# Modulation tiles in pairs between the main products of a two-layer streaming encoder, at half as many places

## The chip, the cores and the metric

The kernel runs on one core of one Trainium2 chip. The metric is device time in microseconds (us), from start to end of one launch, as the median of several runs. Inputs and weights lie in the chip's memory (HBM) at the start, outputs at the end.

## The reference

One inference step of two layers over 288 positions (256 of a prompt, 32 of a running stream), 2048 channels, float32. Each layer begins with a normalization whose shift, scale and gate are computed from a condition vector `c`; that computation is the modulation:

```python
def _adaln(x, c, g, w_mod, b_mod):
    mod = jax.nn.silu(c) @ w_mod + b_mod
    shift, scale, gate = jnp.split(mod, 3, axis=-1)
    h = _rmsnorm(x, g) * (1.0 + scale[:, None, :]) + shift[:, None, :]
    return h.astype(x.dtype), gate[:, None, :]

def _attention_layer(x, c, l, ...):
    h, gate = _adaln(x, c, p['norm_g'][l], p['w_mod'][l], p['b_mod'][l])
    proj = h @ p['w_in_att'][ia]
    ...
    x = x + gate * (mixed @ p['w_out_att'][ia])

def _ssm_layer(x, c, l, ...):
    h, gate = _adaln(x, c, p['norm_g'][l], p['w_mod'][l], p['b_mod'][l])
    u, z = jnp.split(h @ p['w_in_ssm'][isd], 2, axis=-1)
    ...
    glu = g * jax.nn.sigmoid(g @ p['w_glu'][isd] + p['b_glu'][isd])
    out = (glu.astype(x.dtype) * jax.nn.silu(z)) @ p['w_out_ssm'][isd]
    x = x + gate * out
```

`w_mod` is 2048 x 6144 for each layer, 96 MB in all, and is multiplied with only two vectors (one for the prompt, one for the stream). The other weight matrices are multiplied with 288 columns each.

## The kernel before

All weights pass through SBUF in tiles of 1 MB (128 x 4 x 512 floats). Two kinds of tiles run on TensorE, and one list, `jobs`, fixes their order:

- A **main** job (`main_job`, L575) multiplies one tile of a weight matrix with the activations. Since float32 weights are too exact for the fast format, each quarter of a tile is split: ScalarE rounds it (`hi`), VectorE forms the rest (`lo`), and TensorE makes three matmuls of 288 columns for each block (`ah,hi`, `al,hi`, `ah,lo`), 48 in all for a tile. The splitting runs ahead of the multiplying by at most `NQ = 8` quarters (`split_step`, L416; `rest_step`, L436).
- A **mod** job (`mod_jobs`, L569) multiplies one tile of `w_mod` with the condition vectors, in plain float32 and without a split: four products that use 32 columns of the array each, side by side (`mod_mm`, L470), recorded as 8 matmuls. 16 such tiles, or 4, form a group that sums into one PSUM bank `mod_ps`. After the last one `mod_fin` (L532) copies the bank out, turns it by 32 small matmuls and adds the bias.

`run_jobs` (L474) walks the list. For a main job it issues the matmuls of the tile, and after every second block it lets quarters be split and takes up to three steps of side work; for a mod job it issues the products, gives the buffer free and takes up to three steps of side work. The order of the loads is that of the list as well: `pump` (L391) issues the next load on SP's queue as soon as one of `NST = 4` buffers is free (the first stage has three more, the last products one more). A mod tile's buffer is free when its products are done, a main tile's when VectorE has formed the last `lo`.

All else, that is attention, the building of the state-space matrices, normalizations and scans, is side work: generators in `Tasks` (L199) whose steps are laid between the matmuls. Whether a step is due is decided while the program is built, from a `Plan` (L39) that adds up estimated durations for each engine and each transfer. On the chip nothing is reordered: every engine, and SP's queue, takes its instructions in the order in which they were laid.

The stages as the list has them: 8 steps `u` with the first three or four attention projections and the modulation of layer 0 in runs of four tiles (L1344); 36 main jobs of the other attention projections (L1365), side by side with attention and with the builder of the state-space matrices; 16 of the output projection (L1408); 32 of the state-space input, without modulation tiles (L1791); 16 of `w_glu` (L1829) and 16 of `w_out_ssm` (L1841). The modulation tiles not needed at once are held in two lists, which the loops of these stages use up:

```python
late = mod_jobs(0, 8, 9, 10, 11) + mod_jobs(1, 0, 1, 2, 3) + mod_jobs(1, 4, 5, 6, 7)   # L1339
last_mods = [j for s in range(8, 12) for j in mod_jobs(1, s)]                          # L1340
```

Four of the 48 tiles in `late` are laid in the last of the 8 steps `u`; the other 44 follow one by one behind the main jobs of L1365 (36) and of the output projection (8). The 16 of `last_mods` follow one by one behind two of every three main jobs of the last two products. Gates of layer 0 are needed first in `op_evac` (L1379), shift and scale of layer 1 in `h1_task` (L1499), and its gates in `fin_evac` (L1821), a quarter of the channels at a time.

Of the kernel before, what the change touches and what calls it, by code (L numbers as in the profile page):

```python
# [271 lines left out]
def build(tc, I, O):  # L272
# [8 lines left out]
    with ExitStack() as ctx:  # L281
# [54 lines left out]
        def need(*keys):  # L336
            side.until(lambda: all(k in ready for k in keys))
# [47 lines left out]
        jobs = []  # L385
# [183 lines left out]
        def mod_jobs(l, *units):  # L569


            m = dict(l=l, s=units, ps=None, begun=set())
            return [dict(kind="mod", mod=m, i=i, src=I["w_mod"][l, units[i // 4], i % 4]) for i in range(4 * len(units))]

        def main_job(wname, block, c, group, stage, first=None, last=None, wide=False, **kw):  # L575

            return dict(kind="main", group=group, chunk=c, stage=stage, src=I[wname][block, c], wide=wide,
                        first=c == 0 if first is None else first, last=c == 3 if last is None else last, **kw)

        def new_group(evac):  # L580
            return dict(ps=[None] * 8, evac=evac)
# [323 lines left out]
        def qkv_evac(kind, b, after):  # L905
            def ev(n, ps, c):
                if n == 0:
                    need(("read", "f", after))
                    qkv_tile(kind, b)
                act.activation(qkv[kind, b][:, n, :], ps, AF.Copy, scale=0.125 if kind == "qd" else 1.0)  # L910
                if n == 3:
                    ready.add((kind, b))
            return ev

        def z_evac(base):
            def ev(n, ps, c):
                k = base + n
                t = sc.tile([128, T], F32, tag="zt", name="zt")
                act.activation(t, ps, AF.Tanh, scale=0.5)
                dve.scalar_tensor_tensor(MX[:, k, :], t, 1.0, ps, op0=ALU.add, op1=ALU.mult)  # L920
                if n == 3:
                    ready.add(("sz", base // 4))
            return ev
# [415 lines left out]
        late = mod_jobs(0, 8, 9, 10, 11) + mod_jobs(1, 0, 1, 2, 3) + mod_jobs(1, 4, 5, 6, 7)  # L1339
        last_mods = [j for s in range(8, 12) for j in mod_jobs(1, s)]  # L1340
# [3 lines left out]
        for u in range(8):  # L1344
            part = starts[:3 + u % 2]
            nxt = mod_jobs(0, u + 1) if u < 7 else late[:len(part)]
            if u == 7:
                late = late[len(part):]
# [16 lines left out]
        for oi, (kd, b) in enumerate(order):  # L1365
            g = new_group(z_evac((0 if kd == "zf" else 8) + 4 * b) if kd[0] == "z" else
                          qkv_evac(kd, b, 0 if oi < 7 else 1))
            for c in range(4):
                jobs.append(main_job("w_in_att", 2 * ATT.index(kd) + b, c, g, "h0"))
                if oi == len(order) - 1:  # L1370
                    jobs[-1]["key"] = ("free", "h0", c)
                jobs += late[:1]
                late = late[1:]

        def op_evac(gi):
            def ev(n, ps, c):
# [31 lines left out]
        for gi, c in [(gi, c) for gi in range(4) for c in range(3)] + [(gi, 3) for gi in range(4)]:  # L1408
            jobs.append(main_job("w_out_att", gi, c, og[gi], "m0", first=c in (0, 3), last=c in (2, 3)))
            if gi == 0:  # L1410
                jobs[-1]["before"] = (lambda c: lambda: need(("m0", c)))(c)
            if gi == 3:
                jobs[-1]["key"] = ("free", "m0", c)
            jobs += late[:1]
            late = late[1:]
        op1 = len(jobs)

        def x_in(gi):
# [386 lines left out]
        def glu_evac(gi):  # L1805
            def ev(n, ps, c):
                k = 4 * gi + n
                need(("sz1", k))
                t = sl.tile([128, T], F32, tag="zt%d" % (k % 2), name="gt")
                act.activation(t, ps, AF.Tanh, scale=0.25, bias=hbglu[:, k:k + 1])  # L1810
                dve.scalar_tensor_tensor(t, t, 1.0, U[:, k, :], op0=ALU.add, op1=ALU.mult)
                TT(SZ[:, k, :], t, SZ[:, k, :], ALU.mult)
                if n == 3:
                    sp.dma_start(MX[:, 4 * gi:4 * gi + 4, :], x1d[:, 4 * gi:4 * gi + 4, :])
                    ready.add(("glu", gi))
            return ev

        def fin_evac(gi):
            def ev(n, ps, c):
                k = 4 * gi + n  # L1820
                need(("mod", 1, 8 + gi))  # L1821
                xk = MX[:, k, :].rearrange("p (s j) -> p s j", s=LC)
                for b, (j0, j1) in enumerate(((0, JP), (JP, NJ))):
                    dve.scalar_tensor_tensor(xk[:, :, j0:j1], ps.rearrange("p (s j) -> p s j", s=LC)[:, :, j0:j1],
                                             gate[:, 1, k, b:b + 1], xk[:, :, j0:j1], op0=ALU.mult, op1=ALU.add)
                squares(k, MX[:, k, :])
            return ev

        for gi in range(4):  # L1829
            g = new_group(glu_evac(gi))  # L1830
            for c in range(4):
                jobs.append(main_job("w_glu", gi, c, g, "g"))
                if gi == 0:
                    jobs[-1]["before"] = (lambda c: lambda: need(("g", c)))(c)
                if gi == 3:
                    jobs[-1]["key"] = ("free", "g", c)
                if 4 * gi + c > 2 and (4 * gi + c) % 3 < 2:
                    jobs += last_mods[:1]
                    last_mods = last_mods[1:]
        l1c = len(jobs)  # L1840
        for gi in range(4):  # L1841
            g = new_group(fin_evac(gi))
            for c in range(4):
                jobs.append(main_job("w_out_ssm", gi, c, g, "m1"))
                if gi == 0:
                    jobs[-1]["before"] = (lambda c: lambda: need(("m1", c)))(c)
                if (4 * gi + c) % 3 < 2:
                    jobs += last_mods[:1]
                    last_mods = last_mods[1:]
        l1d = len(jobs)  # L1850

        side.add(rstd1_task())
# [178 lines left out]
```

## Time and profile before

| what | value |
|---|---|
| median of three runs | 1312.3 us |
| the three runs | 1311.82, 1312.3, 1322.78 us |
| the profiled execution | 1324.34 us, of which the span from first to last instruction is 1322.4 us |
| mean granted clock of TensorE | 0.976 |
| VectorE, ScalarE busy | 69%, 45% of the span |
| moved by DMA | 334.55 MB, mean 253 GB/s |
| matmuls of the main products, by form | 3 x 2304 records, about 300 ns each, started some 0.134 us apart |

A row of a group or of a timeline names the line of the helper that issues the instruction (always L116 here), the engine, the operation, what it writes and reads by the program's names, its shape, and how many instructions it joins. In a timeline the first number is the start in us from the begin of the span, the second the duration, and the brackets at the end hold the idle time of the engine before it and what ended it. PE is TensorE, PEld its weight loads, DVE VectorE, ACT ScalarE; a name with q is the queue that issues transfers. Matmuls overlap in the array, so that costs on TensorE are read from the starts and not from the durations. In a row of windows the stretch and its length are followed by the busy time of each engine, the granted clock, the busy share of the DMA engines and the GB/s.

### The profile page before, as it was taken

What the parts mean: (1) busy time and instruction counts of PE and PEld (TensorE: products, weight loads), DVE (VectorE), ACT (ScalarE), POOL (GpSimd) and SP (SyncE); (2) the same over time, 40 slices, a digit from 0 to 9 for tenths busy, and PEclk for the clock granted to TensorE, in tenths of its full rate; (3) what the DMA queues carried; (4) which work ended last, traced back from release to release, by engine and by line L of the source; (5) the groups of instructions that cost most, each with busy time, mean ns of one, the idle gap of its engine ahead of it and who ended that gap; (6) DMA issues with size and microseconds to landing.
All of it is one profiled execution on the core that took longest, in us unless ns stands there. A gap on an engine that the chain in (4) does not pass through costs nothing.

```text
span 1322.4 us, 27713 instructions
## 1 busy us (share of the span) xinstructions
PE 1245.6 (94%) x11098; PEld 1106.7 (84%) x11098; DVE 912.3 (69%) x2000; ACT 595.2 (45%) x1398; POOL 31.0 (2%) x20
## 2 busy tenths in 40 slices
PE   4999899998999999999999989998999999999996
PEld 2788688887788788877889987987889999999895
DVE  5569987797787779877764883736767685455554
ACT  4533233243354545554653463433536684344441
POOL 0006000000000000000000000000000000000000
PEclk8899999999999999999999989998999999999998
DMA  9878487577978888878966477588756757777631
GB/s 347 369 290 344 184 309 283 190 278 276 314 291 320 305 325 313 327 268 281 358 226 250 129 272 209 163 241 200 220 170 204 218 178 255 254 259 273 228 124 72
DMA packets 114159, 334.55 MB, mean 253 GB/s; under 512 B 47696, under 2 KB 64096, under 8 KB 83312
## 3 DMA queue, kind: packets, MB, share of 16 engines
q1 hardware_dynamic: 101360, 303.14, 66.3%
q10 hardware_dynamic: 12672, 29.65, 6.0%
q8 instruction: 87, 1.43, 0.4%
q14 instruction: 40, 0.33, 0.1%
HBM read 297.69 MB, written 35.06 MB: 252 GB/s over the span
## 4 chain that ended last, share of the span: by engine, by line
issue 48%; PE 25%; DMA 14%; DVE 10%; ACT 1%; SPq 1%; ACTq 0%; POOL 0%; POOLq 0%; DVEq 0%
PE m L116 19%; DMA w<-in_w_in_att 5%; DMA v_d<-v 5%; PE mod_ps L116 3%; DVE v L116 3%; DVE lo L116 2%; DVE tmpv L116 1%; DMA w_d<-W 1%; DMA w<-in_w_wide 1%; DVE dtmp L116 1%; DMA w<-in_w_mod 1%; DVE MX L116 1%; ACT hi L116 1%; SPq L116 1%; PE w_ps L116 1%
## 5 line engine op out<-in xcount | busy, mean ns | idle before, releaser
L116 PE MATMUL m<-ah,hi 128*128 128x288 f32 (+1 forms) x2304 | 713.5, 310 | 12.3 <-DVE qkv L116 6.0
L116 PE MATMUL m<-ah,lo 128*128 128x288 f32 (+1 forms) x2304 | 688.4, 299 | 5.5 <-DVE lo L116 5.4
L116 PE MATMUL m<-al,hi 128*128 128x288 f32 (+1 forms) x2304 | 689.1, 299 | 3.6 <-DVE al L116 3.6
L116 PEld LDWEIGHTS m<-ah,hi 128*128 128x128 f32 x2304 | 440.9, 191 | 74.4 <-issue 39.9
L116 ACT CAST hi<-w 128x512 fp32r<-128x512 f32 x552 | 322.0, 618 | 350.1 <-PE m L116 220.2
L116 DVE TENSOR_TENSOR lo<-w,hi 128x512 fp32r<-128x512 f32 x552 | 366.8, 686 | 148.9 <-ACT hi L116 146.6
L116 PEld LDWEIGHTS m<-ah,lo 128*128 128x128 f32 x2304 | 441.7, 192 | 7.4 <-DVE lo L116 7.3
L116 PEld LDWEIGHTS m<-al,hi 128*128 128x128 f32 x2304 | 442.1, 192 | 4.1 <-DVE al L116 3.8
L116 PE MATMUL mod_ps<-w,cs 128*32 128x512 f32 x744 | 96.9, 614 | 13.5 <-DVE ssq L116 12.6
L116 DVE SCALAR_TENSOR_TENSOR qkv<-m,qkv 128x288 f32<-128x288 f32 x168 | 72.8, 452 | 26.6 <-PE m L116 26.5
L116 DVE TENSOR_TENSOR v<-pt,raw 128x512 f32<-128x512 f32 (+1 forms) x64 | 46.0, 719 | 29.0 <-DMA v_d<-v 24.0
L116 DVE SCALAR_TENSOR_TENSOR MX<-m,gate,MX 128x256 f32<-128x256 f32 x96 | 30.8, 362 | 30.3 <-PE m L116 30.1
L116 PEld LDWEIGHTS mod_ps<-w,cs 128*32 128x32 f32 x744 | 17.0, 109 | 38.9 <-issue 21.4
L116 DVE TENSOR_TENSOR tmpv<-pt,raw 128x512 f32<-128x512 f32 (+1 forms) x64 | 45.9, 717 | 0.0
L116 ACT ACTIVATE yx<-MX 128x288 f32<-128x288 f32 (+1 forms) x38 | 18.8, 495 | 50.9 <-DVE MX L116 50.4
L116 PE MATMUL t_ps<-MX,kb 32*32 32x288 f32 (+7 forms) x1024 | 40.1, 306 | 0.0
L116 PEld LDWEIGHTS t_ps<-MX,kb 32*32 32x32 f32 x1024 | 27.9, 107 | 12.5 <-issue 2.9
L116 DVE SCALAR_TENSOR_TENSOR MX<-MX,c_dT,t_ps 128x288 f32<-128x288 f32 x16 | 8.2, 514 | 42.8 <-PE t_ps L116 42.8
L116 DVE TENSOR_TENSOR v<-v,tmpv 128x512 f32<-128x512 f32 (+1 forms) x48 | 34.3, 714 | 1.7
L116 PE MATMUL y_ps<-Xm,v 128*128 128x74 f32 x256 | 31.9, 279 | 2.6 <-ACT Xm L116 2.6
L116 PEld LDWEIGHTS y_ps<-Xm,v 128*128 128x128 f32 x256 | 30.8, 196 | 3.1 <-ACT Xm L116 2.8
L116 PE MATMUL w_ps<-c_ident,v 128*128 128x128 f32 x128 | 20.4, 283 | 10.4 <-ACT hi L116 2.1
(236 smaller groups left out, 930.4 us busy)
## 6 DMA issues: line engine op xcount, KB each, us to landing
w<-in_w_mod SPq DMA_DIRECT2D x93, 1024.0 KB, 6.0
w<-in_w_in_att SPq DMA_DIRECT2D x40, 1024.0 KB, 8.3
w<-in_w_in_ssm SPq DMA_DIRECT2D x32, 1024.0 KB, 5.9
w<-in_w_wide SPq DMA_DIRECT2D x24, 1024.0 KB, 10.5
w<-in_w_out_att SPq DMA_DIRECT2D x16, 1024.0 KB, 7.1
w<-in_w_glu SPq DMA_DIRECT2D x14, 1024.0 KB, 5.7
w<-in_w_out_ssm SPq DMA_DIRECT2D x12, 1024.0 KB, 5.0
v_d<-v ACTq DMA_DIRECT2D x16, 576.0 KB, 8.7
```

Of the source, the lines that this page charges most:

```text
L116: return f(*a, **k)
```

## The change

The tiles of `late` that remain after the first stage, and those of `last_mods`, are laid two at a time, behind every second main job of the attention projections and the output projection, and behind one of three in the last two products. Which tiles there are, their order among themselves, and all other work stay.

```diff
@@ attention projections (L1368)
                 jobs.append(main_job("w_in_att", 2 * ATT.index(kd) + b, c, g, "h0"))
                 if oi == len(order) - 1:
                     jobs[-1]["key"] = ("free", "h0", c)
-                jobs += late[:1]
-                late = late[1:]
+                if c % 2:
+                    jobs += late[:2]
+                    late = late[2:]
@@ output projection (L1408)
-            jobs += late[:1]
-            late = late[1:]
+            if len(jobs) % 2:
+                jobs += late[:2]
+                late = late[2:]
@@ w_glu (L1829)
-                if 4 * gi + c > 2 and (4 * gi + c) % 3 < 2:
-                    jobs += last_mods[:1]
-                    last_mods = last_mods[1:]
+                if 4 * gi + c > 2 and (4 * gi + c) % 3 == 1:
+                    jobs += last_mods[:2]
+                    last_mods = last_mods[2:]
@@ w_out_ssm (L1841)
-                if (4 * gi + c) % 3 < 2:
-                    jobs += last_mods[:1]
-                    last_mods = last_mods[1:]
+                if (4 * gi + c) % 3 == 1:
+                    jobs += last_mods[:2]
+                    last_mods = last_mods[2:]
```

Written out with M for a main job and m for a modulation tile, the attention projections go from `M m M m M m M m` to `M M m m M M m m`. The list has 138 entries when the output projection begins, so its first main job makes the count odd, and its pairs stand behind its first, third, fifth and seventh main job. In the last two products the pairs stand behind the main jobs 4, 7, 10 and 13 of `w_glu` and 1, 4, 7 and 10 of `w_out_ssm`, counted from 0; before, single tiles stood behind 3, 4, 6, 7, 9, 10, 12, 13, 15 and 0, 1, 3, 4, 6, 7, 9.

## The prediction

> **What bounds the kernel now.** I read the page first, for the busy shares, then the busy time by stage, alone and for the modulation's matmuls (tile mod_ps).
>
> ```profile
> span 1322.4 us, 27713 instructions
> PE 1245.6 (94%) x11098; PEld 1106.7 (84%) x11098; DVE 912.3 (69%) x2000; ACT 595.2 (45%) x1398; POOL 31.0 (2%) x20
> L116 PE MATMUL mod_ps<-w,cs 128*32 128x512 f32 x744 | 96.9, 614 | 13.5 <-DVE ssq L116 12.6 <-DMA w<-in_w_mod 1.0
> ```
>
> TensorE is busy in 94% of the span, so time taken off TensorE is time gained wherever nothing else ends last. The next rows give all engines in three stages; the rows behind the dots give the modulation's matmuls alone.
>
> ```profile
> core 0: us, PE busy (x) PEld busy (x) DVE busy (x) ACT busy (x) POOL busy (x), PEclk, DMA share, GB/s
> 265.00:680.00 415.00, 395.38 (x3309) 334.01 (x3309) 327.85 (x675) 202.65 (x533) 6.00 (x9) 0.99 0.83 301
> 680.00:706.00 26.00, 26.00 (x197) 22.82 (x200) 14.03 (x28) 11.30 (x24) 0.70 (x1) 1.00 0.76 279
> 1100.00:1270.00 170.00, 170.00 (x1349) 153.22 (x1347) 89.19 (x162) 71.75 (x130) 0.00 (x0) 1.00 0.70 250
> ...
> 265.00:680.00 415.00, 43.11 (x320) 0.99 0.83 301
> 680.00:710.00 30.00, 4.26 (x32) 1.00 0.73 262
> 1100.00:1270.00 170.00, 17.04 (x128) 1.00 0.70 250
> ```
>
> A modulation tile is 8 matmuls, so the last three rows hold 320/8 + 32/8 + 128/8 = 40 + 4 + 16 = 60 tiles: exactly those that the change moves. In the last stage and in the short one TensorE never pauses. In the attention stage (265 to 680) it idles 415 - 395.4 = 19.6 us, while the DMA engines are 83% busy: two resources are near their limit there.
>
> **What a lone tile costs, and a row of four.** The TensorE timeline around a lone tile in the last stage, then around a run of four that the first stage already has:
>
> ```profile
> 1114.42 0.29 PE L116 MATMUL m<-ah,lo 128*128 128x288 f32 x1
> 1114.64 1.06 PE L116 MATMUL mod_ps<-w,cs 128*32 128x512 f32 x8
> 1115.63 0.40 PE L116 MATMUL m<-ah,hi 128*128 128x288 f32 x1
> 1115.87 0.29 PE L116 MATMUL m<-al,hi 128*128 128x288 f32 x1
> ...
> 1116.94 0.29 PE L116 MATMUL m<-ah,hi 128*128 128x288 f32 x1
> ...
> 93.89 0.29 PE L116 MATMUL m<-ah,lo 128*128 128x288 f32 x1
> 94.11 3.64 PE L116 MATMUL mod_ps<-w,cs 128*32 128x512 f32 x32
> 97.68 0.40 PE L116 MATMUL m<-ah,hi 128*128 128x288 f32 x1
> 97.92 0.29 PE L116 MATMUL m<-al,hi 128*128 128x288 f32 x1
> ```
>
> Main matmuls start every (1116.94 - 1115.87)/8 = 0.134 us. From the last one before the tile to the second after it pass 1115.87 - 1114.42 = 1.45 us instead of 2 x 0.134, so a lone tile costs 1.18 us. The run of four costs 97.92 - 93.89 - 0.27 = 3.76 us. Each tile behind the first therefore costs (3.76 - 1.18)/3 = 0.86 us: the other 0.32 us belong to leaving the main product and coming back, whatever the number of tiles.
>
> **The change part by part.** No instruction is added or taken away. Moved are 60 tiles, each one load of 1 MB on SP's queue and 8 weight loads and 8 matmuls on TensorE; POOL gets nothing.
>
> *Fewer crossings.* 60 places become 30: 18 in the loop over the attention projections, 4 in the output projection, 8 in the last two products. A pair costs 1.18 + 0.86 = 2.04 us where two lone tiles cost 2.36. Of 0.32 x 30 = 9.6 us, some is shared already, because a small side product sometimes stands right beside a tile and crosses with it. Going through the TensorE timeline from 265 us on I find 17 of the 60 tiles so placed; the first and the last of them:
>
> ```profile
> 271.84 1.07 PE L116 MATMUL mod_ps<-w,cs 128*32 128x512 f32 x8
> 272.84 0.55 PE L116 MATMUL vt_ps<-c_ident,qkv 128*128 128x128 f32 x3
> ...
> 664.09 0.85 PE L116 MATMUL pv_ps<-VR,PT 128*128 128x128 f32 x6
> 664.87 1.07 PE L116 MATMUL mod_ps<-w,cs 128*32 128x512 f32 x8
> ```
>
> If meetings go with the number of places, half of the 17 are lost and about 8 crossings return (2.6 us); if they go with the number of side steps, which stays, none is. So TensorE saves 7.0 to 9.6 us. All 17 lie in the attention stage; I take 1.3 us as lost, in the middle. Term by term: last two products 8 x 0.32 = 2.6; output projection 4 x 0.32 = 1.3; attention 18 x 0.32 - 1.3 = 4.5 us.
>
> *What of it lies on the path.* In the last stage and in 680 to 706 TensorE has no idle time, so 2.6 + 1.3 = 3.9 us come off the end. In the attention stage, work saved on TensorE can turn into waiting for a tile. A main tile is loaded, then rounded on ScalarE (hi), then its rest is formed on VectorE (lo), then multiplied. One such passage, by the queue and engine timelines:
>
> ```profile
> 547.87 0.64 SPq L116 DMA_DIRECT2D w<-in_w_in_att  x1
> 559.47 2.19 ACT L116 CAST hi<-w 128x512 fp32r<-128x512 f32 x4 [1.10 <-DMA w<-in_w_in_att]
> 565.47 2.67 DVE L116 TENSOR_TENSOR lo<-w,hi 128x512 fp32r<-128x512 f32 x4
> 569.42 0.40 PE L116 MATMUL m<-ah,hi 128*128 128x288 f32 x1
> ...
> 342.49 9.32 DMA w<-in_w_in_att
> ...
> 604.97 9.48 DMA w<-in_w_in_att
> ```
>
> From issue to use pass 21.5 us, and landing (11.6 us) plus splitting fill all but the last 1.3 us of them. The last two rows are the first and the last of seven such loads that the chain of waits runs through between 342 and 605 us. Where that chain runs through a load or VectorE, a shorter TensorE brings nothing. Nothing gained would be 0, all gained 4.5; the stage is 95% TensorE but its chain is broken seven times by loads, so I take half: 2.2 us.
>
> *SP's queue.* The loads go in the order of the jobs, so M m M m becomes M M m m. A tile's buffer is freed by its own matmuls, a main tile's by its last lo. With four buffers, a main's load is issued two mains and two modulation tiles before its use in either order (by hand: both about 20 us ahead when a main takes 9 us and a tile 1). What differs is what goes out with it: the first main of each pair now follows two modulation loads at once, where it followed one. One load more is 1.049 MB at 301 GB/s = 3.5 us. Main loads land in 8.3 us at the median:
>
> ```profile
> w<-in_w_mod SPq DMA_DIRECT2D x93, 1024.0 KB, 6.0
> w<-in_w_in_att SPq DMA_DIRECT2D x40, 1024.0 KB, 8.3
> v_d<-v ACTq DMA_DIRECT2D x16, 576.0 KB, 8.7
> ```
>
> That is 11.8 us for the first main and less than 8.3 for the second, of some 20 us ahead; the rounding of 2.19 us and lo of 2.67 still fit. I cost it at nothing except at one seam: the last pair of the attention loop and the first of the output projection have a single main between them, four tiles around one main. Between 0 and one load time of 3.5 us; 1.0 us taken, since the loads before it are two mains ahead.
>
> *Results that come later.* The groups of tiles that end in the attention loop do so at the same main as now, the one that ends in the output projection one main sooner, and two in the last product one main later, each still at least four mains (4 x 48 x 0.134 = 26 us) before its gate is needed: nothing.
>
> *The planner.* The side work is laid between the main products at build time by estimated times, so from the first pair on every later place may shift. This has no price in the trace. Bounds: all 19.6 us idle of the attention stage gone, or as much again. I take 0, as I know of no reason for either sign.
>
> Sum: 2.6 + 1.3 + 2.2 - 1.0 = 5.1 us off. The profiled execution took 1324.34 us (span 1322.4), so it would take 1319; the median of the runs is 1312.3, 12 us less than the profiled one, and one of three runs lies at 1322.78. Against the median: 1307 us.
>
> **Rivals.**
>
> *The bunched loads starve TensorE (slower).* If the first main of a pair is late by the 3.5 us of the load put ahead of it wherever the chain already goes through such a load, that is 7 x 3.5 = 24.5 us, and 3.9 + 4.5 = 8.4 saved: 1312.3 + 16 = 1328. It eats the gain from the third place on, and passes 1% from the seventh. For it: the 1.3 us that were left at 569.42. Against: the second main of each pair gets earlier by as much. A long stall is also paid twice, as the timeline shows at the one already there:
>
> ```profile
> 318.36 0.69 DVE L116 TENSOR_TENSOR v<-pt,raw 128x512 f32<-128x512 f32 x1 [5.67 <-DMA v_d<-v]
> ...
> 321.04 0.61 PE L116 MATMUL m<-ah,lo 128*128 128x288 f32 x1 [3.48 <-DVE lo L116]
> 321.44 0.44 PE L116 MATMUL m<-ah,hi 128*128 128x288 f32 x1
> 321.68 0.44 PE L116 MATMUL m<-al,hi 128*128 128x288 f32 x1
> ...
> 323.97 0.37 PE L116 MATMUL m<-al,hi 128*128 128x288 f32 x1
> ```
>
> After 3.48 us without work the matmuls start 0.24 us apart instead of 0.134 until 323.97: some 1.3 us more. The Trainium skill, TensorE: Matmul & The Clock Gate, HAM oscillation, says that idle gaps longer than about 3.4 us throttle the array to half its clock; the trace agrees with 0.24 us at this place, and by that rule seven stalls of 3.5 us would cost up to 7 x 1.3 = 9 us more, 1337 in all.
>
> *Full saving and shorter stalls (faster).* VectorE stood 5.67 us for the write v_d, and TensorE for lo behind it.
>
> ```profile
> DVE v L116 <- DMA v_d<-v: 24.0, 8, 5.7
> ```
>
> If the new order of loads leaves that write free, the 3.48 + 1.3 us of that stall go too; with 9.6 saved in full, 1312.3 - 14.4 = 1298. Against: the write goes out on ScalarE's queue beside loads that keep the DMA engines 83% busy in any order. The Trainium skill, DMA: Bandwidth & Descriptors, Queues, rings and completion order, states that each DMA engine takes turns between queues packet by packet; by that rule the write isn't behind the loads of SP's queue at all, so bunching them would neither help nor hurt it. No run here shows this directly.
>
> *The crossings come back.* A side step follows each tile, also inside a pair. If planner and waits give the side products new places of their own and the attention stage is bound by its loads, little is left: 1312 (1310 to 1316).
>
> **How the numbers follow.** My forecast (1300 to 1310) has 0.45, the crossings coming back 0.22, starving 0.17, the faster case 0.16. Faster than 1299.2 is the last (0.16), slower than 1325.4 the third (0.17), the rest 0.67: 1% is about what a measurement of this kernel can tell, whose three runs spread over 0.8%. The range reaches from 1295, under the faster case's 1298, to 1324, so that the starving case (1328, 0.17) and a far end of the faster one (some 0.03) stay out; the forecast alone would be 1300 to 1310.
>
> **What would show it.** The modulation's matmuls stand in runs of 16 from 265 us on, and a pair alone costs 2.04 us between main starts: that proves the first step. Their busy time (1.06 us alone, 3.64 for four, so 1.92 for two) falls by 30 x 0.20 = 6 us from 100.1. The last two products get shorter by 2.6 us: that proves the second. In the attention stage idle TensorE of about 22 us supports the half taken; 35 or more, with waits of hi for w<-in_w_in_att above all at first mains of a pair, is the starving rival. Wrong I would be if the first stage or the state-space stage, where no tile moves, changed by more than 5 us: then the planner decides, not the crossings.

## The result and the profile after

| | median | runs | profiled execution | its span |
|---|---|---|---|---|
| before | 1315.83 us | 20 | 1324.34 us | 1322.4 us |
| after | 1324.78 us | 20 | 1324.46 us | 1322.7 us |

The ratio is 1.0059 with a 95% interval of 1.0045 to 1.0072: the change made the kernel 0.6% (8 us) slower. The forecast was 1307 us, 5 us faster than the median it started from; the time lies just beyond the upper end of the range (1324). One execution of after took 5962.52 us at a granted clock of 0.185 and is left out of the ratio and its interval; without it the median is 1324.75 us.

Three lines of the page of after, then its windows for all engines and, in the last row, for the instructions on mod_ps alone (its matmuls first):

```profile
span 1322.7 us, 27730 instructions
PE 1239.2 (94%) x11098; PEld 1106.2 (84%) x11098; DVE 912.9 (69%) x2000; ACT 594.8 (45%) x1398; POOL 31.1 (2%) x20
L116 PE MATMUL mod_ps<-w,cs 128*32 128x512 f32 x720 | 90.7, 615 | 12.5 <-DVE ssq L116 12.4
```

```profile
265.00:680.00 415.00, 390.55 (x3275) 332.09 (x3274) 325.05 (x671) 202.01 (x537) 6.70 (x10) 0.98 0.81 300
680.00:710.00 30.00, 30.00 (x256) 26.60 (x255) 15.16 (x32) 9.59 (x17) 0.00 (x0) 1.00 0.79 284
1100.00:1270.00 170.00, 170.00 (x1366) 158.23 (x1365) 91.57 (x165) 73.04 (x131) 0.00 (x0) 1.00 0.69 250
...
265.00:680.00 415.00, 40.73 (x320) 7.76 (x320) 1.17 (x2) 0.98 0.81 300
```

The execution of before that the prediction used was itself 8 us above the median of its kernel. The same kernel was therefore profiled once more (the experiment before_again, span 1315.2 us, close to the median); comparisons from here on are with that one. Its row for the attention stage:

```profile
265.00:680.00 415.00, 401.19 (x3365) 339.37 (x3364) 330.15 (x684) 206.60 (x545) 6.71 (x10) 0.99 0.85 306
```

TensorE idles 415 - 401.2 = 13.8 us of this stage in before_again and 415 - 390.6 = 24.4 us in after, and does 90 matmuls fewer in it. This idle time differs from execution to execution: in the four whose loop is laid like that of the kernel before (before, before_again, out_only, tail_only) it is 13.8 to 19.6 us, in the three with pairs loaded in the order of the change (after, att_only, att_even) 23.9 to 26.9. Where the time goes is seen best from the start of the first matmul of each main job, counted from 0 (main 28 is the first of the attention loop and 64 the first of the output projection; from 72 to 110 no tile moves; the tiles of the last two products follow), worked out from the trace:

```
us from ... to ...    28-64   64-72   72-110  110-end   main 36   main 45
before (on record)    369.6    74.0    361.7    253.9      11.9      12.3
before_again          362.4    73.8    363.9    253.9      10.4      11.6
after                 373.4    74.9    365.0    250.7      16.8      20.4
```

The last two products are 3.2 us shorter. The attention loop is 11.0 us longer, of which main 36 and main 45 alone make 6.4 + 8.8 = 15.2. The rest of the loop gained some 4 us. The 11.0 is the largest such difference, since before_again has the shortest of the four like loops (362.4 to 369.6 us); the two mains stand out from all four, which have 9.8 to 11.9 us at main 36 and 10.9 to 13.2 at main 45.

What happens in main 45 of after is seen in three timelines, of SP's queue, of ScalarE and VectorE, and of TensorE:

```profile
399.86 0.99 SPq L116 DMA_DIRECT2D w<-in_w_mod  x2
402.74 0.33 SPq L116 DMA_DIRECT2D w<-in_w_in_att  x1
...
407.79 0.33 SPq L116 DMA_DIRECT2D w<-in_w_in_att  x1
408.57 0.33 SPq L116 DMA_DIRECT2D Fb<-Fp_d  x1
420.30 0.33 SPq L116 DMA_DIRECT2D w<-in_w_mod  x1
420.68 0.43 SPq L116 DMA_DIRECT2D CK<-in_kfT  x1
421.16 0.52 SPq L116 DMA_DIRECT2D Fk<-Fs_d  x1
421.78 0.70 SPq L116 DMA_DIRECT2D w<-in_w_mod  x1
422.58 0.39 SPq L116 DMA_DIRECT2D w<-in_w_in_att  x1
```

```profile
419.56 0.68 DVE L116 TENSOR_TENSOR lo<-w,hi 128x512 fp32r<-128x512 f32 x1
...
441.12 1.14 ACT L116 CAST hi<-w 128x512 fp32r<-128x512 f32 x2 [9.34 <-DMA w<-in_w_in_att]
442.16 0.36 ACT L116 COPY VR<-vt_ps 128x256 f32<-128x256 f32 x1
442.43 0.25 ACT L116 COPY VS<-vt_ps 32x128 f32<-32x128 f32 x1
```

```profile
420.50 1.92 PE L116 MATMUL mod_ps<-w,cs 128*32 128x512 f32 x16
...
442.73 1.11 PE L116 MATMUL w_ps<-c_ident,v 128*128 128x128 f32 x4 [5.73 <-ACT VS L116]
...
444.52 0.44 PE L116 MATMUL m<-al,hi 128*128 128x288 f32 x1
...
445.48 0.44 PE L116 MATMUL m<-ah,lo 128*128 128x288 f32 x1
```

The reader is to follow one pair. Its two tiles are loaded at 399.86 and multiplied only at 420.50, so that for 20 us they hold two of the four buffers. The other two go to mains at 402.74 and 407.79. Then SP issues nothing for 11.7 us, until the last lo of a main at 419.56 sets a buffer free. The first two buffers go to the next two modulation tiles, which TensorE multiplies only at 447 and 450 us; main 46's load, for which ScalarE stands ready from 431.8 on, goes out behind them at 422.58. Between them go CK and Fk, two loads of the side work (1 MB and 272 KB), which had been standing in SP's queue behind the same wait. So 3.3 MB are issued ahead of main 46's tile within 2.3 us, and ScalarE, which stands 9.34 us at its hi, is released only at 441.12. That CK fell into this place is a matter of how the side work was laid; in before_again it goes out at 408.44, with one modulation load in front of it.

TensorE is still in main 45 and doesn't need the tile before 451. But the copies VR and VS stand behind that hi in ScalarE's order, and a small side product on TensorE waits for VS: 5.73 us. The wait is paid for a second time: behind it the matmuls start (445.48 - 444.52)/4 = 0.24 us apart where 0.134 is usual, and the granted clock is 0.50 from 443 to 447 us.

The waits of TensorE in the attention stage and the output projection (265 to 706 us: total, times, longest), after:

```profile
PE m L116 <- DVE lo L116: 7.5, 6, 3.0
PE w_ps L116 <- ACT VS L116: 5.7, 1, 5.7
PE w_ps L116 <- DVE v L116: 4.1, 4, 2.4
```

and before_again:

```profile
PE w_ps L116 <- DVE zs L116: 2.9, 1, 2.9
PE w_ps L116 <- DVE v L116: 2.6, 3, 1.9
...
PE m L116 <- DVE lo L116: 0.6, 2, 0.4
```

Waits for lo rose from 0.6 to 7.5 us, of which main 36 has 6.2, and the one for VS in main 45 is new. Together these two mains wait 12.0 us, about as much as TensorE's idle time grew (10.6).

### The profile page after: what moved, and what is told of

It is laid out like the page before. It is cut to its first block, busy times and chain, and to the rows that moved or that the text cites. A ratio compares the mean times of both kernels' runs of the same rounds, so it can differ in the third digit from the quotient of the medians.

```text
span 1322.7 us, 27730 instructions
## 1 busy us (share of the span) xinstructions
PE 1239.2 (94%) x11098; PEld 1106.2 (84%) x11098; DVE 912.9 (69%) x2000; ACT 594.8 (45%) x1398; POOL 31.1 (2%) x20
## 4 chain that ended last, share of the span: by engine, by line
issue 49%; PE 31%; DMA 10%; DVE 7%; ACT 2%; SPq 1%; POOL 0%; ACTq 0%; POOLq 0%; DVEq 0%
PE m L116 23%; DMA w<-in_w_in_att 5%; PE mod_ps L116 4%; DVE lo L116 2%; DMA w<-in_w_out_att 1%; DVE v L116 1%; DMA w<-in_w_mod 1%; DMA v_d<-v 1%; DMA w<-in_w_wide 1%; PE w_ps L116 1%; DVE MX L116 1%; ACT hi L116 1%; DVE tmpv L116 1%; PE pv_ps L116 1%; SPq L116 1%
## 5 line engine op out<-in xcount | busy, mean ns | idle before, releaser
L116 PE MATMUL m<-ah,lo 128*128 128x288 f32 (+1 forms) x2304 | 687.4, 298 | 10.2 <-DVE lo L116 10.1
L116 DVE TENSOR_TENSOR lo<-w,hi 128x512 fp32r<-128x512 f32 x564 | 374.2, 686 | 158.9 <-ACT hi L116 149.6
L116 ACT CAST hi<-w 128x512 fp32r<-128x512 f32 x564 | 328.4, 618 | 330.8 <-PE m L116 223.6
L116 PE MATMUL mod_ps<-w,cs 128*32 128x512 f32 x720 | 90.7, 615 | 12.5 <-DVE ssq L116 12.4
L116 ACT COPY W<-w_ps 128x512 f32<-128x512 f32 x32 | 18.7, 584 | 32.7 <-PE w_ps L116 32.7
```

The source lines that it names most:

```text
L116: return f(*a, **k)
```

## The experiments

Each kernel is compared with the kernel before, run beside it on the same chip.

| kernel | median, us | before, us | ratio | 95% interval |
|---|---|---|---|---|
| before_again | 1317.22 | 1318.72 | 0.9998 | 0.9975 to 1.0022 |
| tail_only | 1318.33 | 1318.72 | 0.9980 | 0.9955 to 1.0005 |
| out_only | 1319.68 | 1318.72 | 1.0006 | 0.9981 to 1.0031 |
| att_only | 1329.63 | 1318.72 | 1.0075 | 1.0048 to 1.0103 |
| att_even | 1330.17 | 1317.78 | 1.0092 | 1.0067 to 1.0118 |
| att_mainfirst | 1316.59 | 1317.78 | 0.9981 | 0.9966 to 0.9997 |
| after_mainfirst | 1312.36 | 1317.78 | 0.9957 | 0.9935 to 0.9979 |
| before_mainfirst | 1328.16 | 1317.78 | 1.0072 | 1.0044 to 1.0100 |
| before_modfirst | 1374.16 | 1319.14 | 1.0416 | 1.0398 to 1.0434 |
| before_mainfirst_x | 1319.39 | 1316.87 | 1.0010 | 0.9992 to 1.0028 |
| after_mainfirst_x | 1309.97 | 1316.87 | 0.9955 | 0.9932 to 0.9978 |
| after_two_places | 1326.14 | 1318.35 | 1.0044 | 1.0023 to 1.0064 |

**Which part of the change.** Three kernels make one part each of the change: att_only the pairs of L1368, out_only those of L1408, tail_only those of L1829 and L1841, with the lines of the diff shown. Where the pairs of the attention loop stand alone, the rest of `late` follows one by one as before. before_again is the kernel before, unchanged.

> Pairs in the attention projections alone (18 of the 30 pairs). Bunched loads: the first main tile of a pair is loaded behind two modulation tiles and TensorE waits for it, so this part alone makes the kernel slower by about 10 us (the 8 us measured plus the 2.6 us that the last two products should have gained), with waits of hi for w<-in_w_in_att up and the loss between 265 and 680 us. Planner shift: the loss comes from side work that fell on other places, anywhere after 265 us; between 0 and 8 us slower. Crossings only: 4 us faster.

> Pairs in the output projection alone (4 pairs). Bunched loads: single tiles ahead of it, so no seam of four tiles around one main; between 1 us faster and 2 us slower. Planner shift: any difference shows in the state-space stage behind 760 us, where no tile moves. Crossings only: 1.3 us faster.

> Pairs in the last two products alone (8 pairs). TensorE is never idle there, so both the crossings and the bunched loads expect 2.6 us faster, all of it between 1100 and 1280 us. Planner shift: not faster.

> The kernel before once more, for a second profile of it and to see how far two timings of one program lie apart: 0 us, within 2 us; the profiled one of before was 8 us above the median of its runs, a second one should lie nearer to it, with the difference in the first 265 us.

The attention loop alone makes the kernel 0.75% slower; the other two parts are not told from no change. By the ratios the parts are worth +9.9, +0.8 and -2.6 us, +8.1 in sum, and the whole change measured 0.0059 x 1315.8 = +7.8. So they add up within their intervals, and the loss belongs to the 18 pairs of the attention loop. before_again agrees with its 0 us, but not with its guess that the two profiles would differ in the first 265 us: up to main 28 they take 263.2 and 261.3 us, and the loop 369.6 and 362.4. In att_only the same two mains are long as in after: main 36 takes 17.5 us and main 45 20.0. The second is the passage shown, with the same load; the first is seen in the timelines of ScalarE, VectorE and TensorE:

```profile
329.64 1.14 ACT L116 CAST hi<-w 128x512 fp32r<-128x512 f32 x2 [5.68 <-DMA w<-in_w_in_att]
...
330.29 0.69 DVE L116 TENSOR_TENSOR lo<-w,hi 128x512 fp32r<-128x512 f32 x1 [5.85 <-ACT hi L116]
```

```profile
333.28 0.40 PE L116 MATMUL m<-ah,lo 128*128 128x288 f32 x1 [1.57 <-DVE lo L116]
336.01 0.61 PE L116 MATMUL m<-ah,lo 128*128 128x288 f32 x1 [2.07 <-DVE lo L116]
340.10 0.61 PE L116 MATMUL m<-ah,lo 128*128 128x288 f32 x1 [3.00 <-DVE lo L116]
```

Here the late main is the one that TensorE is in. ScalarE stands 5.68 us for its load and VectorE 5.85 for that hi; from then on VectorE works without a long pause, on lo and on the side work laid between, and TensorE stands three times for lo, 6.6 us in all.

**The places, or the order of the loads.** If it is the order of the loads, it can be mended without touching the order of the main and modulation products. att_mainfirst is att_only with this edit in `pump` (L391), and behind the two loops:

```diff
+        load_of = {}
         def pump():
             while pos["load"] < len(jobs):
-                k = pos["load"]
+                k = load_of.get(pos["load"], pos["load"])
...
         op1 = len(jobs)
+        for k in range(rest0, op1 - 2):
+            if [jobs[k + i]["kind"] for i in range(3)] == ["mod", "mod", "main"]:
+                load_of.update({k: k + 2, k + 1: k, k + 2: k + 1})
```

The products are laid as M M m m M M m m, but the load of the main behind a pair is issued ahead of the pair's own two loads. after_mainfirst does the same to the whole change. before_mainfirst does it to the single tiles of the kernel before (m M loaded as M m). att_even is att_only with `c % 2 == 0` in place of `c % 2`, which moves every pair by one main.

Loads are all that such an edit names, but not all that it changes. The plan counts transfers too, so it lays the side work anew. Worked out from the traces for TensorE between main 28 and main 72, some 160 pieces of side products each: 159 of 159 stand behind the same main matmul in before and before_again, 21 in att_only and att_mainfirst, and 18 in before_again and after. (The change itself keeps all other work, but not its places.)

> Pairs in the attention projections as in att_only, but wherever a main tile stands behind two modulation tiles in the list its load is issued ahead of theirs; the order of the products stays. Bunched loads: the first main tile of each pair lands about two transfers (2 x 3.5 us) earlier, so the 10 us lost go and the crossings' gain shows: between 4 us faster and 2 us slower than before, and main 46 no longer starts 20 us behind main 45. Planner shift: the order of loads is not the cause, so it stays some 10 us slower, or moves by chance to either side.

> The kernel before with single tiles, each main tile's load issued ahead of the modulation tile before it: control for the order of loads alone. Bunched loads: one transfer earlier for every main tile, but few waits there now; 0 to 4 us faster. Planner shift: by chance, up to 8 us to either side.

> Pairs in the attention projections behind the first and third main of each group of four instead of the second and fourth: as many places, other side work beside them. Bunched loads: the same hold of two of four buffers through two mains, so again slower, by 5 to 15 us. Planner shift: as likely faster as slower.

> The changed kernel with all its 30 pairs, loads of main tiles ahead of the two modulation tiles in the attention and output projections. Bunched loads: att_mainfirst's result less the 2.6 us of the last two products; between 7 us faster and 1 us slower than before. Planner shift: 8 us slower as the changed kernel, or by chance elsewhere.

With the loads reordered (and the side work laid to suit) the same pairs cost nothing: 1.0075 became 0.9981, and the whole change 0.9957, 0.4% faster than before and the fastest kernel so far. Moving the pairs by one main without reordering (att_even, 1.0092) did not help. The waits of hi for these loads in the attention stage (total, times, longest), in att_only:

```profile
ACT hi L116 <- DMA w<-in_w_in_att: 40.5, 10, 9.5
```

and in att_mainfirst:

```profile
ACT hi L116 <- DMA w<-in_w_in_att: 8.9, 7, 3.3
```

The sum alone would mislead: before_again has 55.7 us of such waits in 17 pieces of at most 7.7, and is faster. It seems that many short ones are hidden by work laid ahead and few long ones are not; no run tests this alone.

before_mainfirst is a miss: expected up to 4 us faster, it came out 0.7% slower. It is taken up below.

**Only the order of the loads.** before_modfirst keeps the order of all main and modulation products of the kernel before and only exchanges the loads the other way, each modulation tile's ahead of the main before it:

```diff
+        for k in range(rest0, op1 - 1):
+            if (jobs[k]["kind"], jobs[k + 1]["kind"]) == ("main", "mod"):
+                load_of.update({k: k + 1, k + 1: k})
```

> The kernel before, single tiles at their old places, but each modulation tile's load issued ahead of the main tile's before it, so that modulation tiles hold more of the four buffers for longer. No place and no crossing changes. Bunched loads (buffers held by modulation tiles keep main tiles from being loaded): slower, by 5 to 20 us, between 265 and 680 us. Crossings or chance: within 3 us of before.

It lost 4.2%, 55 us, far more than the 5 to 20 expected, with no crossing added or removed. The attention loop alone takes 420.7 us in place of 362.4, and TensorE waits mostly for lo:

```profile
PE m L116 <- DVE lo L116: 36.5, 21, 6.5
```

So an edit of the loads' order cost some six times the 9.6 us that all crossings are worth. The side work is laid anew here as well (10 pieces of 159 keep their place), so not all of it need be the loads' own. How the mains' loads land, over mains 30 to 63, is worked out here by counting the packets on SP's queue as if they came in order. That is a reconstruction, its means good to about 1 us and fit for comparing kernels only: at main 46 of after it gives 438.0 where ScalarE was released at 441.1.

```
us, mean              issue to landing    landing to first matmul   least
                      even     odd        even     odd              (even)
before_again           7.8     6.7        11.9     12.5              4.4
att_only               8.5     7.2        11.0     16.7              1.8
after                  8.4     7.0        10.9     16.5              2.6
att_mainfirst          5.3     6.9        20.5     15.5             13.6
before_mainfirst       5.9     6.1        18.4     17.8             13.3
before_modfirst        5.3     5.1         7.1      5.9              1.3
```

Even mains are the first behind a pair. In att_only the pairs make them land 0.7 us later on average, a fifth of the 3.5 us of the rival, and give 4 us to the odd ones. The least margin falls from 4.4 to 1.8. With the main's load first no even main has less than 13.

**Why being early did not help the singles.** before_mainfirst stands 17.5 us ahead of before_again at main 65 (616.3 against 633.8 us) and 3.2 behind at main 67. Two rows of SP's timeline and one of TensorE's waits (600 to 700 us) show what lies there:

```profile
639.26 0.33 SPq L116 DMA_DIRECT2D MX<-in_xP  x1
639.64 0.43 SPq L116 DMA_DIRECT2D CK<-in_kdT  x1
```

```profile
PE Ss L116 <- DMA CK<-in_kdT: 7.0, 1, 7.0
```

MX's buffer was in use until then (SP waited 11.6 us for VectorE's al), and CK, which was free to go, stood behind it. Two kernels move the loads of MX to GpSimd's queue:

```diff
-            sp.dma_start(MX[:, s0_:s0_ + 4, :], I["xP"][:, 4 * gi:4 * gi + 4, :])
+            pool.dma_start(MX[:, s0_:s0_ + 4, :], I["xP"][:, 4 * gi:4 * gi + 4, :])
```

> This is before_mainfirst (the places of the kernel before, each main's load issued ahead of the modulation loads) with one more edit: the loads MX<-in_xP of the query and key source are issued by GpSimd instead of SP. before_mainfirst was 18 us ahead at main 65 and lost it in the two mains behind; there SP's queue held MX<-in_xP until 639.26, with CK<-in_kdT right behind it at 639.64, and PE waited 7.0 us at Ss for CK<-in_kdT. Theory (SP's queue, held by a load whose buffer is not free, is what lost the lead): CK<-in_kdT is issued before 635 and the PE wait at Ss is under 2 us; 9 us or more are recovered, so 0 to 8 us faster than before (ratio 0.994 to 1.000). Rival (the attention's side work itself is not ready earlier, whatever queue its loads stand in): the wait moves to other side work and the time stays 5 to 12 us above before (ratio 1.004 to 1.009).

> This is after_mainfirst (the pairs of the change, each main's load issued ahead of the pair's two modulation loads) with the loads MX<-in_xP issued by GpSimd instead of SP. Theory (SP's queue still delays side loads in the attention): 1 to 4 us faster than after_mainfirst, ratio to before 0.992 to 0.995. Rival (with the pairs SP is not held at these loads, since the mains run less far ahead): within 2 us of after_mainfirst, ratio 0.994 to 0.9975.

CK went out 12.7 us sooner, and TensorE's wait for it is gone from the list:

```profile
626.94 0.43 SPq L116 DMA_DIRECT2D CK<-in_kdT  x1
```

The ratio fell from 1.0072 to 1.0010, some 8 us. The side products stand at the same places in both kernels (160 of 160), so the laying of the side work did not make this difference. It is just short of the 9 asked for, and of the gain over before: 18 us ahead at main 65, this kernel has lost all of it by main 71: mains 64 to 71 take 93.9 us, 73.8 in before_again. What bounds them then was not followed up. With the pairs the move brought nothing that can be measured (0.9957 and 0.9955), as the rival had it.

**Two places, or all of them.** The two long mains explain more than the loss of after. after_two_places reorders the loads at those two pairs alone, before main 36 and before main 46:

```diff
+        mains = [k for k, j in enumerate(jobs) if j["kind"] == "main"]
+        for k in (mains[36] - 2, mains[46] - 2):
+            load_of.update({k: k + 2, k + 1: k, k + 2: k + 1})
```

> The changed kernel with one edit: ahead of two pairs only, those before main 36 and main 46 (counted from 0 in the list), the load of the main is issued ahead of the two modulation loads; the other 20 pairs keep the order of the change. In the changed kernel main 36 takes 16.8 us and main 45 20.5 us (10.4 and 11.6 in the kernel before), and both times ScalarE stands at hi for that main's load (9.34 us at the second). Theory (the change loses its time at these two places, through the late load of the first main of the pair): main 36 takes under 11 us and main 45 under 12.5, ScalarE's longest wait of hi for a load is under 7 us, and the time is 8 to 15 us under that of the change, ratio to before 0.994 to 1.000. Rival (the loss belongs to the order of all pairs: mend one place and the next pair stalls): both mains are mended, others take 5 us or more longer, and the ratio stays at 1.004 or above.

Both mains were mended, and the time was not: 1.0044.

```
us of the main       36      37      45      54      64    28-64   64-72
before_again       10.4     8.9    11.6     9.3    10.1    362.4    73.8
after              16.8    11.6    20.4    10.0    12.9    373.4    74.9
after_two_places    7.6    18.2    11.7    15.1    20.6    365.1    81.9
after_mainfirst     7.3    15.1     9.6     8.7    13.1    353.6    79.7
```

Main 37 now takes 18.2 us, main 64 20.6. Main 54 grew by 5.1 as well. At the first of these ScalarE again stands at the hi of the first main of a pair, 38, and TensorE behind the copy W that follows it:

```profile
349.26 2.17 ACT L116 CAST hi<-w 128x512 fp32r<-128x512 f32 x4 [8.86 <-DMA w<-in_w_in_att]
351.34 0.57 ACT L116 COPY W<-w_ps 128x512 f32<-128x512 f32 x1
```

```profile
351.97 1.12 PE L116 MATMUL w_ps<-c_ident,v 128*128 128x128 f32 x4 [3.74 <-ACT W L116]
```

At the other two it is not a late hi. In main 54 TensorE stands 3.06 us for VectorE's zd, VectorE having stood 4.01 us for a write v_d. In main 64 it stands twice for lo, whose hi were ready at 628.7 and 631.0; VectorE did side work first:

```profile
633.59 0.40 PE L116 MATMUL m<-ah,lo 128*128 128x288 f32 x1 [4.07 <-DVE lo L116]
...
636.12 0.61 PE L116 MATMUL m<-ah,lo 128*128 128x288 f32 x1 [1.75 <-DVE lo L116]
```

So the rival holds in what it forecast, and in part in its reason. With all pairs reordered the ratio is 0.9957, with two of them 1.0044: the other 20 matter. But only one of the three new stalls is that of the next pair's load. A stall comes out wherever the side work, laid anew, happens to stand, and how much of the loss is the loads' and how much this laying's is not settled by these two kernels.

## Why the prediction was wrong

**Fewer crossings: right.** A pair alone costs 2.05 us between main starts, as worked out; one from the last products of after, 1118.91 - 1116.59 - 0.27:

```profile
1116.59 0.30 PE L116 MATMUL m<-ah,lo 128*128 128x288 f32 x1
1116.82 1.06 PE L116 MATMUL mod_ps<-X,cs 128*32 128x512 f32 x8
1117.70 1.04 PE L116 MATMUL mod_ps<-w,cs 128*32 128x512 f32 x8
1118.67 0.40 PE L116 MATMUL m<-ah,hi 128*128 128x288 f32 x1
1118.91 0.30 PE L116 MATMUL m<-al,hi 128*128 128x288 f32 x1
```

Of the 30 pairs in after, 18 stand alone, 5 stand beside a side product, and 7 are divided by one, which the prediction had as a rival and did not count. The modulation's busy time fell by 4.2 us (100.1 to 95.9), not by 6; the 23 undivided pairs make 23 x 0.20 = 4.6. The sums of the modulation's matmuls, before and after:

```profile
sum 880.00, PE 100.14; mean PE 25.03
sum 900.00, PE 95.94; mean PE 23.98
```

**Last two products, -2.6 us: right.** From main 110 to the end after takes 250.7 us against 253.9, tail_only 251.2. The ratio of tail_only alone would not tell it from nothing, but this stretch takes 250.7 to 251.2 us in all five kernels with the pairs there and 253.3 to 254.8 in the nine without.

**Output projection, -1.3 and +1.0: not told apart.** out_only measured +0.8 us with an interval of about -2.5 to +4.1. Main 64, at the seam, took 12.9 us in after and 10.1 before.

**Attention, -2.2: wrong, by about 12 us.** The step that failed is the one on SP's queue, "I cost it at nothing". Its arithmetic on the mean was good: the first main's load is issued 19.3 us ahead of its use in after, 19.6 in before_again, and lands after 8.4 us on average where 11.8 were allowed. Two things were left out. First, it asked whether the tile is there when TensorE wants it ("the rounding of 2.19 us and lo of 2.67 still fit"). But ScalarE takes hi as soon as it was laid, up to eight quarters ahead of TensorE, and holds up every copy behind it; the tile is late when ScalarE reaches it, though TensorE is 10 us away from it (441.12 and 451.1). (Where hi is laid, the plan decides by an estimate of the landing, L416; how far that estimate was off is not on record.) Second, it took each buffer to come free at a steady pace, with one more load going out beside the main's. The pair's two tiles hold half of the buffers until TensorE has passed two mains, SP then issues nothing for 11.7 us, and what had gathered behind that wait, CK and Fk too, goes out ahead of the next main's tile, which took 18.5 us from its issue to ScalarE's release. With the main's load first (att_mainfirst) the loss of the attention pairs is gone: 0.9981 in place of 1.0075. That they are then worth -2.5 us, close to the -2.2 forecast, is no proof of that term, since against before_again the loop takes 4.1 us less there and the eight mains behind it 4.9 more.

The passage at 547.87 was also read a little too tight. Three of the four lo at 565.47 belong to that main, the fourth to the next, so 2.1 us were left and not 1.3; and from 562.9 to 565.5 VectorE did mostly other work, so landing and splitting were not all that filled the time.

**The rivals.** The starving one (1328) had the right resource and place; its size of 3.5 us at each of seven loads was not what the runs showed (0.7 us on average, and a few waits of 5 to 9 us on ScalarE). The test put down for it, 35 us or more of idle TensorE, did not show it either: the idle time rose to 24.4, close to the 22 that were to support the half taken, while the loop got longer. A sign that can be read only to some 6 us (13.8 to 19.6 in executions laid alike) could not decide this. The long stall that is paid twice was right in kind: behind the waits of main 36 the granted clock is 0.50 from 333 to 342 us, and behind that of main 45 as shown. But the limit of 3.4 us for such a stall, as the prediction cites it, is not what these traces show: no single wait in main 36 is longer than 3.0 us, and before_again has the clock at 0.50 from 357 to 360 us behind the wait of 1.9 us for v. The crossings did not all come back, and the faster case did not occur.

**The planner** was taken at 0. The first stage and the stretch from main 72 to 110 moved by 2.6 and 1.1 us, less than the 5 set as the sign of it. Within the attention stage that sign says nothing, and there every edit of pairs or loads lays the side work anew; that share was not measured by itself. The kernels are fewer witnesses than they seem: after and att_only (145 pieces of 160 at the same place) lost 8 and 10 us and att_even, laid otherwise, 12, while att_mainfirst, after_mainfirst and after_mainfirst_x, laid much alike, gained 2.5 to 6 by their ratios. These are two layings against one. What ties the loss of after to its loads is the trace, where the 12.0 us of new waits in main 36 and main 45 lead back to hi and a late load. That the main's load first brings the time back is shown; by how much through earlier landings and by how much through the new laying stays open.

## What to carry to other kernels

When jobs that share a few buffers are regrouped, look at the order of the loads apart from the order of the products: a load whose buffer is held long, for data needed late, is suspect ahead of one whose data must pass two more engines first. (With pairs it paid to turn this round; with single tiles it did not, 1.0072, and 1.0010 with SP's queue cleared.) Measure the slack of a load to the first engine that takes it in order, not to the one at the end of the chain. Count the side loads that gather behind a waiting queue with those that you moved. And do not expect the time back from mending the longest stalls alone: here two were removed, the schedule was laid anew, and others grew.

## What the runs showed of the hardware

**A sequencer that waits holds back what is free to go.** The Trainium skill, DMA: Bandwidth & Descriptors, Issuing engines are not separate DMA queues, says that issuing from several engines saves only the sequencer's time to start a transfer, usually small. The start itself is small here too (0.33 us for MX at 639.26), but it was not all that was saved: in before_mainfirst the queue stood 11.6 us at one load, CK behind it, and another queue for MX was worth some 8 us.

**A stall that one execution has and the next has not.** The prediction showed VectorE standing 5.67 us for the write v_d at 318 us, with the matmuls slow after it. tail_only, whose order of work is the same there, has it too, before_again has not; the rows of VectorE at the same step, first tail_only, then before_again:

```profile
318.99 0.69 DVE L116 TENSOR_TENSOR v<-pt,raw 128x512 f32<-128x512 f32 x1 [5.36 <-DMA v_d<-v]
```

```profile
313.09 0.69 DVE L116 TENSOR_TENSOR v<-pt,raw 128x512 f32<-128x512 f32 x1 [2.06 <-PE mod_ps L116]
```

Four executions whose loop is laid alike (before, before_again, out_only, tail_only) took 369.6, 362.4, 367.2 and 366.5 us from main 28 to 64. So a few us of a single profile of this loop say nothing, and only the ratios over many runs decided here.
